# State-space products in 64-token pieces, and one softmax tail moved behind its gate

## The chip, the cores and the metric

One core of a Trainium2 chip runs the kernel. The metric is device time in microseconds (us) of one launch; lower is better. Engines are named as in the profile: PE multiplies matrices (PEld loads its weights), DVE and ACT do most element-wise work, POOL a little of it, SP issues most DMAs. L12 is line 12 of the kernel.

## What is computed

Two decoder layers on 256 tokens of width 2048, float32. The first is a Mamba-2 mixer, the second sliding-window attention with 32 heads in 4 key groups. Cut to what the change touches, the first layer is:

```python
zxbcdt = x @ w_in                                  # z, xs, B, C, dt
xbc = silu(causal_conv(xbc) + conv_b)              # 64 heads of 64; 8 groups, state 128
da = dt * a                                        # chunks of 128 tokens
decay_in = exp(segsum(da))                         # lower triangle of tokens x tokens
cb = einsum("bcqgn,bcsgn->bgcqs", C, B)
y = einsum("bgcqs,bgrcqs,bcsgrp->bcqgrp", cb, decay_in, xs * dt)  # + the carried state
y = (y + xs * d_skip) * silu(z)
y = y * rsqrt(mean over the group's 512 columns of y*y + eps) * norm_w
x = layernorm(ALPHA * x + y @ w_out)
```

and the second, with q, k, v, gate from projections of x:

```python
p = exp(s - m); p = p / (sum(p) + exp(sink - m))   # window of 128 keys
x = layernorm(ALPHA * x + ((p @ v) * silu(gate)) @ w_out)
```

## The kernel before

Products of activations with weights are done on float32 numbers split into two parts: ACT makes the high part of a weight slice (`wh`, L178), DVE the low part (`wl`, L181), and PE adds three products (L265 for projections, 256 token columns each; L339 for the output products, 512 columns each). These run through nearly the whole kernel, 16 steps to a block of 128 projection columns, with four PSUM buffers in turn (the products with v in layer two take from the same four).

The first layer goes through 8 groups. A group g has ten blocks: B, C, four of xs, four of z. Tables by block number (`plan`, `between`, `beside`) say after which block the small steps of a group are written into the program. A scheduler keeps the relative order where the code pins an instruction, and otherwise sets it. The 256 tokens are treated as one triangle of two 128-token pieces. The steps of a group are:

- `load_decay`: DMAs broadcast the running sums of four heads (a half group) over 128 partitions into `rb`; POOL issues five of them (groups 0 to 2), SP the other eleven.
- `sum_decay`, `exp_decay`: ACT makes the decay `e`, 1536 columns for each half group: eight Relu instructions (L566), one exponential (L573).
- `cb`: PE multiplies B with C (L607, L608); DVE masks it (L609). `by_cb`: DVE multiplies it into `e` (L614).
- `turn_first` (group 0; DVE L629) or `turn_xs`, `carry_xs`, `scale_xs`: xs with tokens on partitions, times dt, in `xd`.
- `ymm`: PE multiplies `xd` with `e` (L670). For each pair of column blocks one PSUM tile is filled and DVE evacuates it into `yz` (L675), then adds the skip term (L681).
- `gate`: POOL multiplies by z, squares, and sums the squares (L686, L688, L692); ACT and DVE split the result (L700, L701). The four blocks go in the order 0, 1, 2, 3. `norm` begins with a sum over partitions on PE (L724).

Layer two goes through `B_ORDER`: q(j), g(j) and o(j) are the query, gate and output products of key group j. Each attends in two halves h. After scores and exponentials (L1248) comes the softmax tail, `rest`: DVE's `weigh` (L1252 to L1255) and the transpose in `turn_far` (L1262), whose result ACT moves for the product with v (L1281). `gate_block` makes four blocks p of a gate: PE, ACT's tanh (L1185), then DVE's product (L1186), which also sets the PSUM buffer free. The tail is written at once, except where the table `BEHIND_HALF` delays it: (3, 0) goes behind the first gate product of its key group.

## Time and profile before

| what | value |
|---|---|
| median of 3 runs (lowest to highest) | 975.44 us (975.06 to 976.07) |
| profiled execution: its own time, its span | 975.83 us, 973.8 us |
| granted clock of PE | 1.00 |
| busy: PE, DVE, ACT, POOL | 99%, 81%, 69%, 12% |
| moved by DMA | 197.90 MB, 203 GB/s |

The profile shows one execution. The 2.0 us between its time and its span lie around the program. PE's matmuls are pipelined: the duration of one is longer than the distance from its start to the next start, so costs on PE are read from starts.

### The profile page before, as it was taken

The page shows a single profiled execution, that of the slowest core. Times are in us where ns is not written, and L with a number is a line of the kernel's source. Part 1 is how long each engine was busy: PE and PEld are TensorE (multiplying, and loading weights), DVE is VectorE, ACT ScalarE, POOL GpSimd, SP SyncE. Part 2 cuts the span into 40 slices and gives each one's busy share as a digit, 9 for nine tenths or more (in the row PEclk, how much of TensorE's full clock was granted, in tenths as well). Part 3 has the DMA queues.
Part 4 walks back from the last instruction along what each step waited for, and adds up shares of the span by engine and source line. Part 5 has one row for each costly group of instructions (what it writes and reads, how often), then busy time and mean ns, then how long its engine had stood idle before and what let it go on. Part 6 is the DMA issues. An engine that isn't in the chain of part 4 may idle for free.

```text
span 973.8 us, 18857 instructions
## 1 busy us (share of the span) xinstructions
PE 965.5 (99%) x7332; PEld 892.0 (92%) x7332; DVE 786.6 (81%) x1217; ACT 671.4 (69%) x1282; POOL 119.1 (12%) x202
## 2 busy tenths in 40 slices
PE   9999999999999999999999999999999999999998
PEld 8999989998999999999899899888999988898976
DVE  7978898896977877787797687889977769778778
ACT  7675884884785686487477579467777776884772
POOL 0000403102110310310300121411000000000002
PEclk9999999999999999999999999999999999999999
DMA  9689467676656666576476654568654545456542
GB/s 359 237 290 337 147 216 228 212 230 203 218 192 220 205 205 206 167 237 213 152 250 203 216 178 155 187 190 265 193 174 158 185 138 186 153 177 213 205 143 86
DMA packets 61273, 197.90 MB, mean 203 GB/s; under 512 B 6800, under 2 KB 11328, under 8 KB 60928
## 3 DMA queue, kind: packets, MB, share of 16 engines
q1 hardware_dynamic: 58528, 188.53, 59.1%
q0 software_dynamic: 2048, 7.65, 2.4%
q8 instruction: 57, 0.93, 0.4%
q10 hardware_dynamic: 608, 0.52, 0.2%
q14 instruction: 32, 0.26, 0.1%
HBM read 194.45 MB, written 2.23 MB: 202 GB/s over the span
## 4 chain that ended last, share of the span: by engine, by line
PE 75%; DVE 10%; ACT 6%; DMA 5%; issue 3%; SPq 1%; DVEq 0%; ACTq 0%
PE mm L265 48%; PE mm L339 20%; DVE wl L181 4%; DMA wr<-in_wa 2%; PE mm L1052 2%; PE ax L670 2%; ACT wh L178 2%; DMA wr<-in_wb 1%; ACT p L1248 1%; DMA xr<-in_first 1%; DVE cv L510 1%; ACT e L566 1%; ACT ptw L1281 1%; ACT pt L1281 0%; DMA rscr<-f 0%
## 5 line engine op out<-in xcount | busy, mean ns | idle before, releaser
L181 DVE TENSOR_TENSOR wl<-wr,wh 128x1024 fp32r<-128x1024 f32 (+2 forms) x354 | 391.5, 1126 | 87.8 <-ACT wh L178 86.0
L178 ACT ACTIVATE wh<-wr 128x1024 fp32r<-128x1024 f32 (+2 forms) x354 | 332.9, 974 | 95.9 <-PE mm L265 50.9
L265 PE MATMUL mm<-xH,wh 128*128 128x256 f32 x1280 | 354.6, 277 | 0.1
L265 PE MATMUL mm<-xH,wl 128*128 128x256 f32 x1280 | 353.8, 276 | 0.0
L265 PE MATMUL mm<-xL,wh 128*128 128x256 f32 x1280 | 353.7, 276 | 0.0
L265 PEld LDWEIGHTS mm<-xH,wh 128*128 128x128 f32 x1280 | 240.3, 188 | 2.3 <-issue 1.0
L265 PEld LDWEIGHTS mm<-xL,wh 128*128 128x128 f32 x1280 | 240.4, 188 | 1.0
L265 PEld LDWEIGHTS mm<-xH,wl 128*128 128x128 f32 x1280 | 240.3, 188 | 0.1
L265 PE MATMUL mm<-x1H,wh 128*128 128x256 f32 x512 | 142.2, 278 | 2.1 <-DVE sg L1186 2.1
L265 PE MATMUL mm<-x1L,wh 128*128 128x256 f32 x512 | 141.6, 277 | 0.0
L265 PE MATMUL mm<-x1H,wl 128*128 128x256 f32 x512 | 141.5, 276 | 0.0
L339 PE MATMUL mm<-wh,yH 128*128 128x512 f32 x256 | 100.8, 394 | 0.1
L339 PE MATMUL mm<-wh,yL 128*128 128x512 f32 x256 | 99.8, 390 | 0.0
L339 PE MATMUL mm<-wl,yH 128*128 128x512 f32 x256 | 99.7, 390 | 0.0
L265 PEld LDWEIGHTS mm<-x1H,wh 128*128 128x128 f32 x512 | 96.1, 188 | 3.6 <-DVE sg L1186 2.4
L265 PEld LDWEIGHTS mm<-x1L,wh 128*128 128x128 f32 x512 | 96.2, 188 | 0.1
L265 PEld LDWEIGHTS mm<-x1H,wl 128*128 128x128 f32 x512 | 96.2, 188 | 0.0
L510 DVE SCALAR_TENSOR_TENSOR cv<-mm,pc,cv 128x255 f32<-128x255 f32 x144 | 68.4, 476 | 4.6 <-ACT cv L508 2.5
L686 POOL TENSOR_TENSOR yz<-yz,z 128x256 f32<-128x256 f32 x32 | 26.7, 843 | 259.2 <-DVE yz L681 259.2
L339 PEld LDWEIGHTS mm<-wl,yH 128*128 128x128 f32 x256 | 48.1, 188 | 10.3
L339 PEld LDWEIGHTS mm<-wh,yH 128*128 128x128 f32 x256 | 48.1, 188 | 9.7 <-issue 0.3
L339 PEld LDWEIGHTS mm<-wh,yL 128*128 128x128 f32 x256 | 48.1, 188 | 9.0
(247 smaller groups left out, 1262.8 us busy)
## 6 DMA issues: line engine op xcount, KB each, us to landing
wr<-in_wa SPq DMA_DIRECT2D x154, 512.0 KB, 5.2
wr<-in_wo SPq DMA_DIRECT2D x64, 512.0 KB, 4.4
wr<-in_wq SPq DMA_DIRECT2D x32, 512.0 KB, 4.4
wr<-in_wg SPq DMA_DIRECT2D x31, 512.0 KB, 4.8
wr<-in_wb SPq DMA_DIRECT2D x16, 512.0 KB, 4.0
wr<-in_wb SPq DMA_DIRECT2D x32, 256.0 KB, 4.3
rb<-rscr SPq DMA_DIRECT2D x11, 512.0 KB, 5.4
wr<-in_wkv SPq DMA_DIRECT2D x8, 512.0 KB, 5.7
```

The costliest lines, as they stand in the source:

```text
L178: m = nc.scalar.activation(h[:, sl], v, AF.Copy)
L181: m = nc.vector.tensor_tensor(l[:, sl], v, h[:, sl].bitcast(F32), ALU.subtract)
L265: m = nc.tensor.matmul(ps, a, b, start=first and i == 0, stop=last and i == 2)
L339: pinned(nc.tensor.matmul(ps, a[:, k, hs], (u.h, u.l)[l][:, ks], start=n == 0 and add is None, stop=n == 11), pin)
L510: nc.vector.scalar_tensor_tensor(a[:, sft:], ps[:, : S - sft], w(3 - sft), a[:, sft:], ALU.mult, ALU.add)
L566: m = nc.scalar.activation(e[:, h, cols], rb[:, h, c * P :], AF.Relu, scale=-1.0, bias=rtk[:, c, h0 + h : h0 + h + 1])
L670: nc.tensor.matmul(ps[64 * r : 64 * r + 64, cols], st.xd[:, c, i, 64 * r : 64 * r + 64], e[:, 256:] if c else e[:, :256], start=c == 0, st ...
L686: nc.gpsimd.tensor_tensor(v, v, st.z[i][:], ALU.mult)
L1052: m = nc.tensor.matmul(ps[:], (x1H, x1L, x1H)[i][:, kk, hs], (u.h, u.h, u.l)[i][:, ks], start=(kk, i) == (0, 0), stop=ui == 3 and (k, i) = ...
L1248: nc.scalar.activation(byhead[:, r], byhead[:, r], AF.Exp, bias=ng[:, r : r + 1], accum_out=rs[:, r : r + 1])
L1281: nc.scalar.copy(to[32 * c : 32 * c + 32].rearrange("p r a -> p (r a)"), src[32 * i : 32 * i + 32, cc_].rearrange("p r b -> p (r b)"),)
```

## The change

The tokens of a group are cut into 64-token pieces c = 0 to 3 for the products with the decay. Piece c meets only the tokens from 64c on, so it has 256, 192, 128 or 64 columns (`PART`).

- `ymm`: 32 matmuls of 64 rows by 64 columns of the PE array instead of 16 of 128 rows by 64. The row half is r (the head pair's upper or lower part of the array), the column half b. Both PSUM tiles, one for each r, are complete only after the last product; DVE evacuates blocks 0 and 2, then 1 and 3. The gates follow in the order 0, 2, 1, 3.
- `cb`: four matmuls instead of two, two masks on 64 partitions by 320 columns instead of one on 128 by 384, and two new POOL copies of 64 by 320 to the other half of the partitions. `by_cb` waits for these.
- `sum_decay`: still eight Relu instructions for a half group, now of 256, 192, 128 and 64 columns. `exp_decay` and `by_cb` go over 1280 columns instead of 1536.
- `load_decay`: two DMAs of 64 partitions instead of one of 128, with half the bytes in all, into own halves of `rb`.
- `turn_dt` (once): four ACT copies instead of one, one small exponential and one small product more. `turn_first`: eight products on 64 partitions instead of four on 128. `carry_xs`: as many copies as before to other places.
- `BEHIND_HALF` holds (2, 0) instead of (3, 0): the tail of the third key group's first half stands behind the first gate product of its key group; that of the fourth is written at once.

The core of the diff:

```diff
+PART = [slice(a, a + 256 - 64 * c) for c, a in enumerate((0, 320, 512, 256))]
-BEHIND_HALF = [(1, 1), (3, 0)]
+BEHIND_HALF = [(1, 1), (2, 0)]
...
     def load_decay(g, hf):
-        rb = ap.tile([P, 4, S], F32, tag="rb", name=nm("rb"), bufs=2)
+        rb = ap.tile([P, 2, 2, S], F32, tag="rb", name=nm("rb"), bufs=2)
...
+        for r in range(2):
+            m = (nc.sync if sp else nc.gpsimd).dma_start(
+                rb[64 * r : 64 * r + 64, 0],
+                rscr[h0 + 2 * r : h0 + 2 * r + 2, :]
...
     def cb(g):
...
-        nc.tensor.matmul(ps[:, :256], st.bt[:, :128], st.ct[:], start=True, stop=True)
-        nc.tensor.matmul(ps[:, 256:384], st.bt[:, 128:], st.ct[:, 128:], start=True, stop=True)
-        nc.vector.tensor_tensor(cbm[:], ps[:, :384], mask_ssd, ALU.mult)
+        for c, half, to in ((0, 0, 0), (1, 64, 0), (2, 64, 192), (3, 0, 256)):
+            nc.tensor.matmul(
+                ps[half : half + 64, to : to + 256 - 64 * c], st.bt[:, 64 * c : 64 * c + 64], st.ct[:, 64 * c :],
+                start=True, stop=True,
+            )
+        for r in range(2):
+            rows, at = slice(64 * r, 64 * r + 64), slice(320 * r, 320 * r + 320)
+            nc.vector.tensor_tensor(cbm[rows, at], ps[rows, :320], mask_ssd[rows], ALU.mult)
+        for r in range(2):
+            rows, at = slice(64 * r, 64 * r + 64), slice(320 * r, 320 * r + 320)
+            nc.gpsimd.tensor_copy(cbm[64 - 64 * r : 128 - 64 * r, at], cbm[rows, at])
...
     def ymm(g):
...
+        pss = [ax_tile(), ax_tile()]
         for k in range(2):
-            ps = ax_tile()
-            for i in (2 * k, 2 * k + 1):
-                o = (i % 2) * S
-                for c in range(2):
-                    cols = slice(o + c * P, o + S)
-                    for r in range(2):
-                        e = es[g, i // 2][:, 2 * (i % 2) + r, :]
+            for c in range(4):
+                for r in range(2):
+                    rows = slice(64 * r, 64 * r + 64)
+                    for b in range(2):
                         nc.tensor.matmul(
-                            ps[64 * r : 64 * r + 64, cols], st.xd[:, c, i, 64 * r : 64 * r + 64], e[:, 256:] if c else e[:, :256],
-                            start=c == 0, stop=c == 1,
+                            pss[r][64 * b : 64 * b + 64, k * S + 64 * c : k * S + S], st.xd[rows, k, b, c],
+                            es[g, k][rows, b, PART[c]], start=c == 0, stop=c == 3,
                         )
...
-        for i in range(4):
+        for i in (0, 2, 1, 3):
             at(y, gate, g, i)
...
-            (behind_gate if j == 3 else halves).append(rest)
+            (behind_gate if j == 2 else halves).append(rest)
```

What this makes of the order is shown at three places. The first is PE at the products of group 0; `ax` are the PSUM tiles, `e` the decay of a half group, `mm` the projection blocks. Before:

```order
L265 MATMUL mm_1251<-xH,wl_1092 128x256
L670 MATMUL ax_1310<-e_792,xd_1150 64x256 x2
L670 MATMUL ax_1310<-e_792,xd_1150 64x128 x2
L670 MATMUL ax_1310<-e_792,xd_1150 64x256 x2
L670 MATMUL ax_1310<-e_792,xd_1150 64x128 x2
L670 MATMUL ax_1322<-e_871,xd_1150 64x256 x2
```

And with the change, on PE at the same place:

```order
L265 MATMUL mm_1270<-xH,wl_1107 128x256
L683 MATMUL ax_1329<-e_800,xd_1165 64x256 x2
L683 MATMUL ax_1330<-e_800,xd_1165 64x256 x2
L683 MATMUL ax_1329<-e_800,xd_1165 64x192 x2
L683 MATMUL ax_1330<-e_800,xd_1165 64x192 x2
L683 MATMUL ax_1329<-e_800,xd_1165 64x128 x2
L683 MATMUL ax_1330<-e_800,xd_1165 64x128 x2
L683 MATMUL ax_1329<-e_800,xd_1165 64x64 x2
L683 MATMUL ax_1330<-e_800,xd_1165 64x64 x2
L683 MATMUL ax_1329<-e_879,xd_1165 64x256 x2
```

The first tile was written by the first half group alone; now both tiles are written by each half group, in four products (two rows) for every piece.

The second place is DVE behind these products, where `cv` is the convolution of the next xs block, `el` the carried-in decay, and `yz` the group's y. Before:

```order
L510 SCALAR_TENSOR_TENSOR cv_1301<-mm_1251,pc,cv_1301 128x255
L675 TENSOR_TENSOR yz_1309<-ax_1310,el_943 128x512
L510 SCALAR_TENSOR_TENSOR cv_1301<-mm_1251,pc,cv_1301 128x254
L681 SCALAR_TENSOR_TENSOR yz_1309<-xs_712,pc,yz_1309 128x256
L510 SCALAR_TENSOR_TENSOR cv_1301<-mm_1251,pc,cv_1301 128x253
L681 SCALAR_TENSOR_TENSOR yz_1309<-xs_786,pc,yz_1309 128x256
L675 TENSOR_TENSOR yz_1309<-ax_1322,el_943 128x512
```

And with the change, on DVE behind the products of group 0:

```order
L511 SCALAR_TENSOR_TENSOR cv_1320<-mm_1270,pc,cv_1320 128x255
L181 TENSOR_TENSOR wl_1474<-wr_1477,wh_1473 128x1024
L511 SCALAR_TENSOR_TENSOR cv_1320<-mm_1270,pc,cv_1320 128x254
L511 SCALAR_TENSOR_TENSOR cv_1320<-mm_1270,pc,cv_1320 128x253
L689 TENSOR_TENSOR yz_1328<-ax_1329,el_951 128x2x256
L517 SCALAR_TENSOR_TENSOR xs_1319<-xs_1319,cv_1320 128x256
L695 SCALAR_TENSOR_TENSOR yz_1328<-xs_715,pc,yz_1328 128x256
L695 SCALAR_TENSOR_TENSOR yz_1328<-xs_870,pc,yz_1328 128x256
L689 TENSOR_TENSOR yz_1328<-ax_1330,el_951 128x2x256
```

The first evacuation stands behind a whole `wl` and all of the convolution.

The third place is DVE at the first gate block of key group 2; `sg` is the gate, `sm` and `p` belong to the softmax. Before:

```order
L181 TENSOR_TENSOR wl_9960<-wr_9961,wh_9959 128x896
L1252 TENSOR_TENSOR sm_9821<-sm_9821 128x8
L1253 RECIPROCAL sm_9821<-sm_9821 128x8
L1254 TENSOR_SCALAR sm_9821<-sm_9821 128x8
L1255 TENSOR_TENSOR p_9808<-p_9808,sm_9821 128x8x4x32
L181 TENSOR_TENSOR wl_9960<-wr_9963,wh_9959 128x1024
L1262 STREAM_TRANSPOSE z_9839<-p_9808 128x1024
L1186 SCALAR_TENSOR_TENSOR sg_9891<-sg_9891,mm_9904 128x256
```

And with the change, on DVE at that gate block:

```order
L181 TENSOR_TENSOR wl_10150<-wr_10151,wh_10149 128x896
L181 TENSOR_TENSOR wl_10150<-wr_10153,wh_10149 128x1024
L1200 SCALAR_TENSOR_TENSOR sg_10079<-sg_10079,mm_10092 128x256
L1266 TENSOR_TENSOR sm_10015<-sm_10015 128x8
L181 TENSOR_TENSOR wl_10289<-wr_10290,wh_10288 128x128
L1267 RECIPROCAL sm_10015<-sm_10015 128x8
L181 TENSOR_TENSOR wl_10289<-wr_10290,wh_10288 128x896
L1268 TENSOR_SCALAR sm_10015<-sm_10015 128x8
L181 TENSOR_TENSOR wl_10289<-wr_10292,wh_10288 128x1024
L1269 TENSOR_TENSOR p_10002<-p_10002,sm_10015 128x8x4x32
L1276 STREAM_TRANSPOSE z_10147<-p_10002 128x1024
```

The gate product now stands ahead of the five instructions of the tail, and the next unit's three `wl` are spread among them.

More of the change, by code (lines that the diff above doesn't have):

```diff
@@ L411, in first_products @@
         return pss
[L414 to L415 removed]
+    dtx = ap.tile([P, NHD // 2, 4], F32, tag="dtx", name="dtx")
+    dtq = ap.tile([P, 2, 2, 8], F32, tag="dtq", name="dtq")
+    rtk = ap.tile([P, 2, 3, 2, NHD // 2], F32, tag="rtk", name="rtk")
     rscr = dram.tile([P, S], F32, tag="rscr", name="rscr")
```

105 lines of the change are left out of this document (53 added, 52 removed).

## The prediction

> **What bounds the kernel now.** I read the page first, then the chain, PE's waits, and the timeline at the places that the change touches.
>
> ```profile
> PE 965.5 (99%) x7332; PEld 892.0 (92%) x7332; DVE 786.6 (81%) x1217; ACT 671.4 (69%) x1282; POOL 119.1 (12%) x202
> PE 75%; DVE 10%; ACT 6%; DMA 5%; issue 3%; SPq 1%; DVEq 0%; ACTq 0%
> L670 PE MATMUL ax<-e,xd 128*64 128x256 f32 x128 | 19.6, 385 | 0.0
> L670 PE MATMUL ax<-e,xd 128*64 128x128 f32 x128 | 12.4, 273 | 0.0
> ```
>
> PE is busy 99% of the span and carries 75% of the chain. DVE (81%) and ACT (69%) have room on the whole, so what they save counts only where PE waits for them. These are PE's waits over the span, by line, releaser, total, times and longest:
>
> ```profile
> PE mm L265 <- DVE sg L1186: 2.1, 1, 2.1
> PE ax L388 <- DVE zero L376: 1.0, 1, 1.0
> PE ax L724 <- POOL sq L692: 0.3, 1, 0.3
> ```
>
> Two of the three lie where the change works: the gate product and the sum of squares. So there are two ways to gain: fewer PE cycles in eight visits to the products, and the 2.1 us wait. There is one evident way to lose, at L724.
>
> **The products on PE.** The timeline of PE at group 1's products and at the attention scores (columns: start, time, operation), the second being the nearest operation with four 64 by 64 tiles:
>
> ```profile
> 141.95 2.82 PE L670 MATMUL ax<-e,xd 128*64 128x256 f32 x32
> 144.70 0.50 PE L339 MATMUL mm<-wh,yH 128*128 128x512 f32 x1
> ...
> 733.35 1.53 PE L1220 MATMUL ax<-kT,qT 64*64 64x192 f32 x32
> 734.81 0.39 PE L265 MATMUL mm<-x1H,wh 128*128 128x256 f32 x1
> ```
>
> Each float32 matmul is two records. A visit to L670 is 32 records; with two column tiles working side by side that makes 16 pairs, eight of 256 and eight of 128 columns, 3072 columns in a row, and lasts 144.70 - 141.95 = 2.75 us. L1220 has 32 records; if four tiles work side by side that is eight quartets of 192, 1536 columns in a row, in 734.81 - 733.35 = 1.46 us. The difference, 1.29 us for 1536 columns, is 0.84 ns a column, and 0.17 us is left for entering and leaving in both. If only pairs overlapped in L1220, its 3072 columns would need 2.75 us as L670 does; so there they do overlap in fours.
>
> The new visit has 64 records, 16 quartets: for each of two k and two passes 256 + 192 + 128 + 64 = 640 columns, 2560 in all. At 0.84 ns that is 2.15 + 0.17 = 2.32 us, 0.43 us less than now. No row has a quartet of 64 columns. The nearest that tells what a short matmul costs is the four one-column matmuls of L724:
>
> ```profile
> 106.45 0.28 PE L265 MATMUL mm<-xH,wl 128*128 128x256 f32 x1
> 106.99 0.61 PE L724 MATMUL ax<-cc,sq 128*128 128x1 f32 x4 [0.26 <-POOL sq L692]
> 107.46 0.68 PE L607 MATMUL ax<-ct,bt 128*128 128x256 f32 x2
> ```
>
> They take 107.46 - 106.99 = 0.47 us, 0.118 each, however few the columns. Were that a floor for a quartet, the four of 64 columns would cost 0.064 more than their 0.054 and the four of 128 columns 0.010 more than their 0.108: 0.30 us a visit, which leaves a gain of 0.13. L724 loads 128 by 128 weights, twice the columns of these tiles, so I take the middle: -0.3 us a visit, between -0.43 and -0.13. In group 0 it is swallowed by the wait below, so seven visits count: -2.1 us (-3.0 to -0.9).
>
> On that floor the Trainium skill, TensorEngine Tiling (Array Packing), Instruction Overhead, speaks against this change: a matmul carries about 60 cycles of overhead on TRN2, one with a free dimension of 1 lasts as long as one with 60, and a tiling factor should not be taken from a dimension that is already small. Pieces of 64 columns are at that limit. The 0.118 us of L724 agrees that short matmuls have a floor; no run here shows it for four tiles.
>
> `cb` streams 256 + 128 columns through the whole array before; after, each column half takes 320 (256 + 64 and 192 + 128), side by side as the pairs of L670. At 0.84 ns that is 0.05 us less, against entering another tile shape (part of the 0.17 above): I take zero.
>
> **The wait at L724.** DVE and POOL behind group 0's products:
>
> ```profile
> 94.14 0.48 DVE L510 SCALAR_TENSOR_TENSOR cv<-mm,pc,cv 128x255 f32<-128x255 f32 x1
> 94.53 0.68 DVE L675 TENSOR_TENSOR yz<-ax,el 128x512 f32<-128x512 f32 x1
> 95.13 0.47 DVE L510 SCALAR_TENSOR_TENSOR cv<-mm,pc,cv 128x254 f32<-128x254 f32 x1
> 95.52 0.47 DVE L681 SCALAR_TENSOR_TENSOR yz<-xs,pc,yz 128x256 f32<-128x256 f32 x1
> ...
> 96.08 0.73 POOL L686 TENSOR_TENSOR yz<-yz,z 128x256 f32<-128x256 f32 x1 [23.47 <-DVE yz L681]
> ...
> 101.48 0.91 POOL L686 TENSOR_TENSOR yz<-yz,z 128x256 f32<-128x256 f32 x1 [0.37 <-DVE yz L681]
> ...
> 106.19 0.74 POOL L692 TENSOR_TENSOR sq<-sq,sq 128x256 f32<-128x256 f32 x1
> ```
>
> POOL's gates begin when the first skip term ends (95.99) and end at 106.93, and PE waits for that: without it L724 would start about 0.11 after 106.45, so 0.42 us are lost now. With the change the first evacuation follows 255 columns of convolution (to 94.53), one `wl` (1.14 from start to start), the 254 and 253 columns (0.39 each), its own 0.60, an xs product (0.35) and the skip term (0.47): 97.9 us, 1.9 later. POOL has 0.37 us of waiting for DVE inside the chain, and DVE's remaining steps come closer together, since both evacuations are ready at once. So I take 0.7 off and 1.2 us for POOL's end and for PE behind it. The bounds are 0, if DVE is through its queue early enough to keep the old start, and 2.2, if nothing is caught up and the extra instructions of `turn_first`, next, still push DVE by 0.3.
>
> `turn_first` issues eight products on half the partitions instead of four:
>
> ```profile
> 81.50 1.41 DVE L629 TENSOR_TENSOR xd<-ax,dtx 128x256 f32<-128x256 f32 x4
> ...
> L609 DVE TENSOR_TENSOR cbm<-ax,cc 128x384 f32<-128x384 f32 x8 | 4.4, 545 | 0.0
> L614 DVE TENSOR_TENSOR e<-e,cbm 128x1536 f32<-128x1536 f32 x16 | 27.9, 1746 | 3.4 <-ACT e L573 3.3
> L573 ACT ACTIVATE e<-e 128x1536 f32<-128x1536 f32 x16 | 23.6, 1478 | 0.0
> L534 POOL DMA_DIRECT2D rb<-rscr x5: 528/545/719, 43.1 to 118.6; - x5
> ```
>
> As each goes over as many columns as before, that adds 1.3 to 1.4 us to DVE once, ahead of the products of group 0. It is the reason for the upper bound above.
>
> **The steps off PE.** By columns, L614 goes from 1746 to 1455 ns, sixteen times, and L573 from 1478 to 1232; the mask of 545 ns becomes two of 320 columns, about 0.47 each, +0.4 us eight times. In groups 2 to 7 none of this counts: PE waits for none of it now, as the list above shows, and the products come several blocks after `e` is ready. The new POOL copies cost 0.5 to 1.0 us each by POOL's nearest rows (the 0.73 and 0.91 of L686 with 128x256), and POOL is busy 12%. The halved `rb` costs one more issue for each load: five more on POOL at 0.55 us, ahead of POOL's gates, and eleven on SP ahead of the weights' loads; both run blocks ahead of the use. `turn_dt`'s extra copies (about 1.4 us of ACT) lie in the DMA-bound start. All zero; if the cover were gone, the largest single step is the two copies, about 1.5 us, in group 1.
>
> Group 1 is where DVE's columns do count:
>
> ```profile
> 130.11 0.28 PE L265 MATMUL mm<-xH,wl 128*128 128x256 f32 x1
> 130.46 0.50 PE L339 MATMUL mm<-wh,yH 128*128 128x512 f32 x1
> ...
> 135.85 0.39 PE L339 MATMUL mm<-wl,yH 128*128 128x512 f32 x1
> 136.31 0.36 PE L265 MATMUL mm<-xH,wh 128*128 128x256 f32 x1
> ```
>
> L265 starts normally follow after 0.11 us and L339 after 0.23; here 0.35 and 0.46, so 0.47 us are lost while DVE is late with z and the layer's sums. DVE saves 0.6 there and adds 0.4, and PE comes later by the wait at L724: -0.4 us (-0.5 to 0).
>
> **The softmax tail.** PE, DVE and ACT at the gate of key group 2:
>
> ```profile
> 832.09 1.48 PE L1220 MATMUL ax<-kT,qT 64*64 64x192 f32 x32
> 831.12 0.17 DVE L1252 TENSOR_TENSOR sm<-sm 128x8 f32<-128x8 f32 x1 [1.49 <-ACT p L1248]
> 832.90 1.22 DVE L181 TENSOR_TENSOR wl<-wr,wh 128x1024 fp32r<-128x1024 f32 x1
> 834.04 1.24 DVE L1262 STREAM_TRANSPOSE z<-p 128x1024 f32<-128x1024 f32 x1
> 835.20 0.38 DVE L1186 SCALAR_TENSOR_TENSOR sg<-sg,mm 128x256 f32<-128x256 f32 x1
> 832.14 0.36 ACT L1185 ACTIVATE sg<-mm 128x256 f32<-128x256 f32 x1
> 859.43 1.23 DVE L181 TENSOR_TENSOR wl<-wr,wh 128x1024 fp32r<-128x1024 f32 x1 [0.71 <-ACT wh L178]
> ```
>
> ACT's tanh is done at 832.50, but the product that frees the first block's PSUM buffer stands behind the tail until 835.20. Two gate blocks and two products with v have taken the four buffers by then, so PE's third block waits for it: the 2.1 us of the list. With the change it follows the `wl` (1.14 from start to start), which can run once ACT's part of it is made, from about 832.0 to 833.2, and ends near 833.6. PE's scores end near 833.5 (832.09 + 1.46). So about 2.0 us of wait go. Late next: behind the product, the tail and the next unit's `wl` share DVE, some 3 us (1.14 + 1.16 + three small ones) later than now. DVE's wait in the last row shows 0.71 us free there; a `wl` standing behind a transpose (1.16), a gate product (0.34) and a mask could keep PE waiting up to 0.7. I take -1.4 us (-2.1 to -0.3).
>
> The tail of (3, 0) is now immediate, in front of a gate product on DVE. That product ended at 904.83; three more us there are covered, since the buffer that it frees is needed only when PE is through the second block, whose tanh follows at 913.91:
>
> ```profile
> 904.42 0.41 DVE L1186 SCALAR_TENSOR_TENSOR sg<-sg,mm 128x256 f32<-128x256 f32 x1
> 913.91 0.38 ACT L1185 ACTIVATE sg<-mm 128x256 f32<-128x256 f32 x1
> ```
>
> **Sum.** -2.1 + 1.2 - 0.4 - 1.4 = -2.7 us on the profiled 975.83, so 973.1. That run was 0.4 above the median of 975.44; from the median it is 972.7. All favourable ends give -3.0 + 0 - 0.5 - 2.1 = -5.6 (969.8), all unfavourable -0.9 + 2.2 + 0 - 0.3 = +1.0 (976.4).
>
> **Rivals.**
> *Only pairs overlap (slower).* L1220's order alternates between row halves, while the new loop goes through the column halves of one row half first. If the four did not overlap, a visit would take 5120 columns at 0.84 ns and 0.17, 4.47 us, 1.72 more than now. Eight visits make +13.8; with the other terms (+1.2 - 0.4 - 1.4) the time is 988.6. It decides from a visit above 2.75 us. For it: no row shows this order. Against: L1220's fours.
> *Short pieces have a floor.* At 0.118 us for a quartet the products gain only 0.9: -0.9 + 1.2 - 0.4 - 1.4 = -1.5, 973.9, within what can be told. The page named above gives this mechanism its reason.
> *Waits take the place of waits.* The sum of squares is late by the full 2.2 and the attention pays back all but 0.3: -2.1 + 2.2 - 0.4 - 0.3 = -0.6, 974.8. For it: both stand in queues without slack. Against: PE's list has just one such wait in the attention.
> That the change does not do what it says I give nothing: the order shows the gate product ahead of the tail.
>
> **Chances.** The forecast has 0.60, the pairs 0.18, the floor 0.11, the swapped waits 0.11. A measurement of this kernel tells about 0.2%, 1.95 us, from no change. So faster 0.60, same 0.22, slower 0.18. The range from 969.8 to 976.4 takes in all the bounds and the two middle rivals, and leaves out the pairs.
>
> **What would show it.** Right: L683 to the next line's start about 2.45 us in each group, L724 starting near 108.2, no wait of PE for sg at 833, and PE's next waits under 1 us. Wrong: visits of 4.5 us (pairs), visits of 2.6 (floor), L724 past 109 or a new PE wait for `wl` near 858 (swapped waits).

## The result: slower by 0.3%

| kernel | median of 7 runs | lowest to highest |
|---|---|---|
| before | 975.23 us | 974.91 to 976.13 |
| changed | 978.05 us | 976.95 to 980.47 |

The ratio is 1.0031 (95% interval 1.0019 to 1.0043). The prediction of 972.7 us, with a range up to 976.4, was wrong, and its sign too. The runs of the changed kernel also spread over 3.5 us, those of before over 1.2. The profiled execution is the slowest of the seven: 980.47 us with a span of 978.7, so it shows more loss than the median.

The page of the changed kernel, busy time first, then the shares of the chain:

```profile
PE 967.8 (99%) x7620; PEld 897.1 (92%) x7620; DVE 786.1 (80%) x1230; ACT 664.9 (68%) x1286; POOL 125.4 (13%) x223
PE 80%; ACT 6%; DVE 5%; issue 4%; DMA 3%; POOL 1%; ACTq 0%; SPq 0%; DVEq 0%; POOLq 0%
```

PE is busy 2.3 us longer although it multiplies fewer columns. PE's waits of the changed kernel (line, releaser, total, times, longest):

```profile
PE ax L738 <- POOL sq L706: 2.7, 1, 2.7
PE mm L339 <- DVE xr L350: 1.9, 1, 1.9
...
PE mm L265 <- DVE wl L181: 0.2, 1, 0.2
```

The wait for `sg` is gone as forecast. The wait for the sum of squares (L724 before, L738 now) has grown from 0.3 to 2.7 us, and a wait of 1.9 us is new: an output product of o(1) (L339) waits for DVE to free a PSUM buffer (L350). PE's timeline in the changed kernel at the places that matter:

```profile
108.11 0.28 PE L265 MATMUL mm<-xH,wl 128*128 128x256 f32 x1
111.08 0.61 PE L738 MATMUL ax<-cc,sq 128*128 128x1 f32 x4 [2.69 <-POOL sq L706]
...
146.85 2.41 PE L683 MATMUL ax<-e,xd 64*64 64x256 f32 x64
149.19 0.51 PE L339 MATMUL mm<-wh,yH 128*128 128x512 f32 x1
...
835.04 1.48 PE L1234 MATMUL ax<-kT,qT 64*64 64x192 f32 x32
836.61 0.39 PE L265 MATMUL mm<-x1H,wh 128*128 128x256 f32 x1
...
880.88 0.39 PE L339 MATMUL mm<-wl,oH 128*128 128x512 f32 x1
883.17 0.57 PE L339 MATMUL mm<-wh,oH 128*128 128x512 f32 x1 [1.90 <-DVE xr L350]
883.54 0.63 PE L339 MATMUL mm<-wh,oL 128*128 128x512 f32 x1
883.97 0.63 PE L339 MATMUL mm<-wl,oH 128*128 128x512 f32 x1
```

A visit to the products lasts 149.19 - 146.85 = 2.34 us. In the last two rows the step from one start to the next is 0.43 us, where the same instruction normally follows after 0.23: behind the wait PE runs at half its clock. The windows of the changed kernel show it behind both waits (window, length, PE busy, granted clock, DMA share, GB/s):

```profile
112.00:118.00 6.00, 6.00 (x26) 0.72 0.57 198
884.00:888.00 4.00, 4.00 (x13) 0.64 0.72 261
```

Time in which PE is busy at 0.72 or 0.64 of its clock is part of why the busy time rose. Set side by side, PE's starts in the two profiled executions give the whole balance; the last column is how far the changed kernel is behind by then:

| PE reaches | before | changed | behind |
|---|---|---|---|
| group 0's products, start | 87.37 | 89.43 | +2.06 |
| group 0's products, end | 90.12 | 91.77 | +1.65 |
| the norm's sum (L724, L738) | 106.99 | 111.08 | +4.09 |
| the first L265 behind it | 113.67 | 119.45 | +5.78 |
| group 1's products, start | 141.95 | 146.85 | +4.90 |
| group 2's products, start | 232.79 | 237.94 | +5.15 |
| group 7's products, end | 613.37 | 616.28 | +2.91 |
| scores at key group 2's gate | 832.09 | 835.04 | +2.95 |
| next L265 | 835.64 | 836.61 | +0.97 |
| last L339 ahead of the new wait | 879.15 | 880.88 | +1.73 |
| end of o(1) | 884.91 | 890.44 | +5.53 |
| last matmul (L1453, L1467) | 967.39 | 971.88 | +4.49 |
| span | 973.8 | 978.7 | +4.9 |

So the two waits with the half clock behind them cost 2.44 + 1.7 and 2.06 + 1.7 us, the way to group 0's products 2.06, and against that stand eight visits at -0.41, -1.98 at the old wait and -0.9 in group 1. That makes +3.8 of the +4.9; the rest is spread (+0.66 between groups 1 and 2, +0.76 between the gate and o(1), +0.7 in small steps, -1.04 near the end).

### The profile page after: what moved, and what is told of

Its sections match the earlier page's. It is cut to its first block, busy times and chain, and to the rows that moved or that the text cites. A ratio compares the mean times of both kernels' runs of the same rounds, so it can differ in the third digit from the quotient of the medians.

```text
span 978.7 us, 19519 instructions
## 1 busy us (share of the span) xinstructions
PE 967.8 (99%) x7620; PEld 897.1 (92%) x7620; DVE 786.1 (80%) x1230; ACT 664.9 (68%) x1286; POOL 125.4 (13%) x223
## 4 chain that ended last, share of the span: by engine, by line
PE 80%; ACT 6%; DVE 5%; issue 4%; DMA 3%; POOL 1%; ACTq 0%; SPq 0%; DVEq 0%; POOLq 0%
PE mm L265 49%; PE mm L339 25%; PE mm L1066 2%; DVE wl L181 2%; ACT wh L178 2%; DMA wr<-in_wa 2%; PE ax L683 2%; DMA xr<-in_first 1%; ACT p L1262 1%; PE ax L610 1%; ACT ptw L1295 1%; ACT pt L1295 0%; DMA first<-in_first 0%; PE ax L1227 0%; PE ax L1234 0%
## 5 line engine op out<-in xcount | busy, mean ns | idle before, releaser
L265 PE MATMUL mm<-xH,wh 128*128 128x256 f32 x1280 | 356.2, 278 | 0.0
L265 PE MATMUL mm<-xL,wh 128*128 128x256 f32 x1280 | 355.1, 277 | 0.0
L265 PE MATMUL mm<-xH,wl 128*128 128x256 f32 x1280 | 355.1, 277 | 0.0
L265 PEld LDWEIGHTS mm<-xH,wh 128*128 128x128 f32 x1280 | 240.9, 188 | 1.9 <-issue 0.3
L265 PEld LDWEIGHTS mm<-xL,wh 128*128 128x128 f32 x1280 | 241.0, 188 | 1.0
L265 PEld LDWEIGHTS mm<-xH,wl 128*128 128x128 f32 x1280 | 241.2, 188 | 0.0
L265 PE MATMUL mm<-x1H,wh 128*128 128x256 f32 x512 | 142.4, 278 | 0.1
L265 PE MATMUL mm<-x1H,wl 128*128 128x256 f32 x512 | 141.8, 277 | 0.2 <-DVE wl L181 0.2
L265 PE MATMUL mm<-x1L,wh 128*128 128x256 f32 x512 | 141.8, 277 | 0.0
L339 PE MATMUL mm<-wh,yH 128*128 128x512 f32 x256 | 101.5, 397 | 0.0
L339 PE MATMUL mm<-wh,yL 128*128 128x512 f32 x256 | 100.4, 392 | 0.0
L339 PE MATMUL mm<-wl,yH 128*128 128x512 f32 x256 | 100.4, 392 | 0.0
L265 PEld LDWEIGHTS mm<-x1H,wh 128*128 128x128 f32 x512 | 96.2, 188 | 1.6 <-issue 0.6
L265 PEld LDWEIGHTS mm<-x1H,wl 128*128 128x128 f32 x512 | 96.3, 188 | 0.4 <-DVE wl L181 0.4
L265 PEld LDWEIGHTS mm<-x1L,wh 128*128 128x128 f32 x512 | 96.2, 188 | 0.1
L714 ACT ACTIVATE yH<-yz,pc 128x256 fp32r<-128x256 f32 x32 | 16.3, 510 | 70.3 <-POOL yz L700 70.3
L339 PEld LDWEIGHTS mm<-wl,yH 128*128 128x128 f32 x256 | 48.4, 189 | 10.2
L339 PEld LDWEIGHTS mm<-wh,yH 128*128 128x128 f32 x256 | 48.5, 189 | 9.8
```

The source lines that it names most:

```text
L265: m = nc.tensor.matmul(ps, a, b, start=first and i == 0, stop=last and i == 2)
L339: pinned(nc.tensor.matmul(ps, a[:, k, hs], (u.h, u.l)[l][:, ks], start=n == 0 and add is None, stop=n == 11), pin)
L714: nc.scalar.activation(yH[:, i, :], v, AF.Copy, scale=pc[:, c : c + 1])
```

## The experiments

Each kernel was timed in 7 to 12 executions beside the kernel before on the same chip, except two that were executed once. There were four such sets, each on another chip; the median of before was 975.33 to 975.46 in all four.

**The two parts alone.** First, before with the softmax tail moved and nothing else:

```diff
-BEHIND_HALF = [(1, 1), (3, 0)]
+BEHIND_HALF = [(1, 1), (2, 0)]
...
-            (behind_gate if j == 3 else halves).append(rest)
+            (behind_gate if j == 2 else halves).append(rest)
```

> The kernel before with the softmax-tail edit alone. If the moved tail is what costs in the output products of key group 1 (waits theory), the wait of 2.4 us on PE before the third gate block of key group 2 goes (-2.0), and a wait of about 2 us on PE for L350 near 879 appears, with PE at part of its clock behind it (another 0 to 1.9): 975.0 to 977.0 in all. If the tail edit does what was forecast and the loss comes from the products (products theory), 973.3 to 974.2, and no such wait.

Measured: 976.63 us (975.48 to 981.57), ratio 1.0022 (1.0011 to 1.0032). The tail's move makes the kernel slower by itself. PE's waits of this kernel:

```profile
PE mm L339 <- DVE xr L350: 1.9, 1, 1.9
...
PE mm L265 <- ACT wh L212: 0.2, 1, 0.2
PE mm L339 <- DVE wl L181: 0.2, 1, 0.2
```

The 2.1 us at the gate became 1.9 us in o(1), some 45 us later, and two small ones. Here the clock stayed full behind the wait:

```profile
879.00:883.00 4.00, 3.77 (x16) 1.00 0.93 298
```

Second, the changed kernel with the old `BEHIND_HALF`, so the pieces alone (the reverse of the diff above):

> The changed kernel with the softmax tails as before, so the 64-token products alone. Waits theory: products -3.3, cb +1.6, the wait at the sum of squares +2.4 and 0 to 1.6 of part clock behind it, group 1 -0.8: 975.1 to 977.0. Rival (four tiles at once draw the clock down everywhere): starts of L265 3% apart from normal in many stretches, 977 or more. If the tail were the only loss: 973 or less.

Measured: 977.51 us (974.13 to 979.57), ratio 1.0030 (1.0019 to 1.0041). So the pieces lose too, and spread over 5.4 us. (The tail alone stays within 2.6 us but for one execution of 981.57.) By the medians the parts cost 1.3 and 2.2 us beside before, and the whole change 2.8. The profiled execution is the fastest of this kernel, 974.13, and its waits have no L738:

```profile
PE mm L265 <- DVE sg L1200: 2.1, 1, 2.1
...
```

**Each once more**, one execution with no edit, to see whether a longer execution differs by that wait. The pieces alone:

> The second run once more, for another profile, since its first profile was its fastest execution. Waits theory: an execution near the median shows the wait at the sum of squares (1.5 to 3 us) and weights landing later near 50 to 60 us than in the first profile.

Measured: 978.54 us, with the wait:

```profile
PE mm L265 <- DVE sg L1200: 2.1, 1, 2.1
PE ax L738 <- POOL sq L706: 1.8, 1, 1.8
...
```

And the changed kernel:

> The changed kernel once more, for another profile. Waits theory: the wait for L350 at the output products of key group 1 is there again, about 2 us; the wait at the sum of squares is 0 to 3 us and goes with the time.

Measured: 976.18 us, without it:

```profile
PE mm L339 <- DVE xr L350: 1.9, 1, 1.9
...
```

Of the four profiled executions of these two kernels, the two with the wait at L738 took 978.54 and 980.47, the two without it 974.13 and 976.18. It comes and goes from run to run in the same program. What varies ahead of it is when DVE comes to group 0's `xd`: 82.98 and 82.59 us in the two profiles with the wait, 79.15 and 78.25 in the two without. Weights that arrive at another time go with that. The last ACT step that waits for a DMA ahead of it started at 60.09 us in the changed kernel (first row) and at 55.38 in the first profile of the pieces alone (second row); in the other two profiles it is 59.71 with the wait and 56.28 without. From 62 to 100 us DVE idles only 2.5 us, so little of such a delay is made up. That the weights are the cause is not shown: in the kernel with the shortened sum, below, DVE came to `xd` late, at 81.97, and ACT's last such wait had ended at 50.88.

```profile
60.09 1.06 ACT L178 ACTIVATE wh<-wr 128x1024 fp32r<-128x1024 f32 x1 [2.26 <-DMA wr<-in_wa]
```

```profile
55.38 1.06 ACT L178 ACTIVATE wh<-wr 128x1024 fp32r<-128x1024 f32 x1 [2.25 <-DMA wr<-in_wa]
```

**Is it DVE's extra work in group 0?** In the pieces alone, PE turns group 0's xs with 16 matmuls against the identity, straight onto the right partitions, so that DVE has two products of 128 by 512 instead of eight on 64 partitions:

```diff
+            for q in range(4):
+                for r in range(2):
+                    nc.tensor.matmul(
+                        ps[64 * r : 64 * r + 64, q * P : (q + 1) * P], st.xs[2 * k + r][:, 64 * q : 64 * q + 64], ident,
+                        start=True, stop=True,
+                    )
+            m = nc.vector.tensor_tensor(st.xd[:, k], ..., ALU.mult)
```

> As the second run, but group 0's xs is turned by PE straight into the new places (sixteen products with the identity, 64 rows each, instead of eight transposes), so DVE needs two products of 128 by 512 instead of eight of 64 by 256, and the small product and exponential for them go. PE pays about 0.9 us for it, DVE saves about 2.1 ahead of group 0's products. Waits theory: the wait at the sum of squares shrinks by about 2 to 0.5-1.0 us and no part clock follows: 1 to 2.5 us below the second run. If DVE's lateness there has another cause, the wait stays above 2 us and the time is 0 to 1 above the second run.

Measured: 975.89 us (975.08 to 976.33), ratio 1.0008 (0.9999 to 1.0017): 1.6 us less than the pieces alone, and the spread is gone. The two sides of the trade, DVE's products in this kernel and in the changed kernel:

```profile
80.83 1.28 DVE L635 TENSOR_TENSOR xd<-ax,dtx 128x512 f32<-128x512 f32 x2
```

```profile
82.98 3.55 DVE L641 TENSOR_TENSOR xd<-ax,dtq 64x256 f32<-64x256 f32 x8
```

The eight products took 3.55 us, where I had put twice the 1.41 of before. One of them lasts as long as one of before (421 and 416 ns on average), but they follow each other at 0.45 us instead of 0.33.

**The lateness without the pieces.** Before, with its four products cut into eight on 64 partitions:

```diff
+                for q in range(2):
+                    rows = slice(64 * q, 64 * q + 64)
-                    st.xd[:, :, i, :]..., ps[:, o : o + S]..., dtx[:, ...]
+                    st.xd[rows, :, i, :]..., ps[rows, o : o + S]..., dtx[rows, ...]
```

> The kernel before with group 0's four products of 128 by 256 on DVE (L629) made as eight of 64 by 256, and nothing else. Waits theory: DVE is 2.1 us later from 83 us on and has no idle time to catch up, so the wait at the sum of squares (L724) grows from 0.4 to about 2 us: 976.5 to 978.5. If the late evacuation order alone made that wait in the changed kernel: 975.2 to 975.8.

Measured: 975.65 us (974.39 to 978.88), ratio 1.0006 (0.9998 to 1.0015). This expectation failed. The eight products lasted 3.52 us here too, but PE's wait stayed as it was:

```profile
PE ax L726 <- POOL sq L694: 0.3, 1, 0.3
```

But POOL's sum did end 0.64 us later than in before (107.57 against 106.93). PE was late by the same 0.64 in this execution, from 20 us on, so the wait did not grow. DVE's 2.1 us reach POOL in part, and alone they made no long wait here. The other half is PSUM tiles that are complete only after the last product, so that the first evacuation comes behind the convolution. In the profiled execution of the changed kernel that is the DVE and then the POOL timeline:

```profile
96.81 0.48 DVE L511 SCALAR_TENSOR_TENSOR cv<-mm,pc,cv 128x255 f32<-128x255 f32 x1
97.20 1.21 DVE L181 TENSOR_TENSOR wl<-wr,wh 128x1024 fp32r<-128x1024 f32 x1
98.34 0.99 DVE L511 SCALAR_TENSOR_TENSOR cv<-mm,pc,cv 128x254 f32<-128x254 f32 x2
99.25 0.68 DVE L689 TENSOR_TENSOR yz<-ax,el 128x512 f32<-128x512 f32 x1
100.22 0.88 DVE L695 SCALAR_TENSOR_TENSOR yz<-xs,pc,yz 128x256 f32<-128x256 f32 x2
```

```profile
100.84 0.86 POOL L700 TENSOR_TENSOR yz<-yz,z 128x256 f32<-128x256 f32 x1 [25.77 <-issue]
109.97 1.06 POOL L706 TENSOR_TENSOR sq<-sq,sq 128x256 f32<-128x256 f32 x1
```

The first evacuation starts at 99.25 instead of 94.53, and POOL's chain at 100.84 instead of 96.08. From there POOL needs 10.19 us to 111.03 where before took 10.85 (96.08 to 106.93), so it makes up 0.66 of 4.76 us; the rest, 4.10, is what the norm's sum starts later on PE.

**Is it that wait?** In the pieces alone, the sum that PE waits for in group 0 holds the first block only, so the sums of the other three squares are missing from the group's normalisation:

```diff
+        elif g == 0 and i == 2:
+            st.rest = q
         else:
-            nc.gpsimd.tensor_tensor(st.ss[:], st.ss[:], q[:], ALU.add)
+            to = st.rest if g == 0 else st.ss
+            nc.gpsimd.tensor_tensor(to[:], to[:], q[:], ALU.add)
```

> The second run, but the sum of squares of group 0 that PE waits for holds the first block alone; the other three are added into a tile that nobody reads (this part of the computation is left out). All of POOL's and DVE's work stays. Waits theory: PE no longer waits there, and the median falls from 977.5 to 974.0-975.5, with a spread as narrow as in the third run. If the wait is not what makes the second run's median and spread: 976.5 to 978.

Measured: 975.79 us (974.65 to 979.12), ratio 1.0007 (0.9998 to 1.0016), 1.7 us below the pieces alone, but with a spread that stayed wide, which the expectation had not. So the wait at the norm, with what follows it, is worth 1.7 us in the median, and does not make the whole spread. In its profiled execution (977.38) DVE's lateness came out elsewhere, at `cv` (the row for `sg` is the old wait at the gate):

```profile
PE mm L265 <- DVE sg L1203: 2.0, 1, 2.0
PE mm L265 <- DVE cv L511: 1.7, 1, 1.7
...
PE mm L339 <- DVE cv L511: 0.6, 1, 0.6
```

**The slow stretches.** Behind `cb` of group 0, PE's L265 follow each other at 117.8 ns instead of 113.4 for some 14 us, at a granted clock of 1.00. The first row is before, the second the changed kernel:

```profile
61.00:76.00 15.00, 15.00 (x135) 1.00 0.73 241
```

```profile
61.00:76.00 15.00, 15.00 (x130) 1.00 0.77 251
```

Fewer matmuls fit into the same full window. The first suspect is `cb` in column halves, so one kernel lets `cb` go over the whole array in two matmuls again, with masks and POOL copies to suit:

```diff
+        nc.tensor.matmul(ps[:, :256], st.bt[:, :128], st.ct[:], start=True, stop=True)
+        nc.tensor.matmul(ps[:, 256:384], st.bt[:, 128:], st.ct[:, 128:], start=True, stop=True)
+        for r, at, of, w in ((0, 0, 0, 384), (1, 384, 64, 192), (1, 576, 320, 64)):
+            ...
+            nc.vector.tensor_tensor(cbm[rows, at : at + w], ps[rows, of : of + w], cc[rows, m : m + w], ALU.mult)
```

> As the second run, but B times C in two products over the whole array as before (256 and 128 columns), masked in three pieces of 384, 192 and 64 columns, with the columns of the decay in another order. If the four small products cost 0.2 us in each of eight groups, 1.6 us below the second run; if not, within 0.3 of it.

Measured: 977.32 us (976.47 to 978.2), ratio 1.0023 (1.0013 to 1.0034), within 0.2 us of the pieces alone; the 1.6 us did not come. The window behind `cb` did become fast, but another one became slow, and DVE's later `cv` cost PE 1.5 us:

```profile
61.00:76.00 15.00, 15.00 (x135) 1.00 0.81 250
44.00:59.00 15.00, 15.00 (x130) 1.00 1.02 327
```

```profile
PE mm L264 <- DVE sg L1195: 2.1, 1, 2.1
PE mm L264 <- DVE cv L510: 1.5, 1, 1.5
...
```

The second suspect is the address from which the next projection step reads its tokens. The program keeps a second copy of the first token tile and reads it between plain blocks, but not behind the places on a list (`visits`). With PE turning xs, this kernel takes `cb` and `turn_first` off that list, so that the step behind them reads the second copy:

```diff
-    visits = (turn_dt, cb, turn_first, ymm, norm)
+    visits = (turn_dt, ymm, norm)
```

> The third run with one more edit: after B times C and after the turning of group 0, the first projection step reads the second copy of the first token tile (at another address), as the kernel does between plain blocks. In the profiles with 64-token pieces whole stretches of L265 (60 to 77, 77 to 90, 178 to 190 us) start 117.8 ns apart instead of 113.4. If which of the two rates a stretch takes is set where it is entered, by the first address, these stretches come back to 113.4 or others turn slow: a change of 0.5 to 1.5 us from the third run. If the four-tile products set it, the stretches stay at 117.8 and the time within 0.3 us.

Measured: 975.93 us (975.09 to 977.32), ratio 1.0007 (0.9999 to 1.0016), the same as with the list. The stretch behind the turning became fast, the one behind `cb` stayed slow. Over all 16 profiles, PE loses 0.83 us against before from 58 to 75 us in each of the eight with `cb` in column halves, 0.25 of it at `cb`, and at most 0.04 in the seven others with `cb` over the whole array. So in group 0 the slow rate comes with the column halves. But it also comes at places without them: between 9 and 19 us it is there in the profile of the next kernel, whose first layer is that of before, and not in before's own. What sets it there stays open.

**Can the tail be moved for less?** Before, with DVE's `weigh` at once and only the transpose behind the gate product:

```diff
+        def part():
+            weigh()
+            behind_gate.append(turn_far)
...
+        elif (j, h) == (2, 0):
+            part()
```

> The kernel before with only the transposes of the tail of (2, 0) behind the gate product; the scaling of p stays ahead of it. Waits theory (the tail's scaling and transposes and the next weights crowd DVE until the output products of key group 1): the wait at the third gate block shrinks by one transpose, 1.2 us, and the transposes come only 0.3 later, so that L350 keeps its place: 974.0 to 974.8. If any delay of the transposes is paid back in full in the output products: 975.0 to 975.6.

Measured: 975.39 us (974.68 to 975.98), ratio 1.0001 (0.9992 to 1.0009):

```profile
PE mm L265 <- DVE sg L1186: 1.4, 2, 0.9
...
PE mm L339 <- DVE xr L350: 0.6, 1, 0.6
```

Half of the move takes 0.7 off the waits for `sg` (2.1 before, now 1.4 in two) and puts 0.6 on L350. The same with the pieces and PE turning xs:

> The third run and the tail split of the sixth together. If the two places are independent the gain of the sixth adds to the third: 974.6 to 975.2; if the tail's gain is paid back: 975.8 to 976.2.

Measured: 976.28 us (975.5 to 977.36), ratio 1.0013 (1.0004 to 1.0021), no better than without it (975.89).

Then POOL instead of DVE scales p of that half, with the transposes behind the gate product; first on before, then on the version below:

```diff
-            nc.vector.tensor_tensor(
+            (nc.gpsimd if (j, h) == (2, 0) else nc.vector).tensor_tensor(
                 byhead, byhead, ri.unsqueeze(2).unsqueeze(3).to_broadcast([P, 8, 4, 32]), ALU.mult
...
+            behind_gate.append(lambda: later(1, turn_far, 0))
```

> The same edit on the kernel before. If the wait is worth its 2.1 us: 973.0 to 974.0; with part clock behind it in some executions of before, more. If it is paid back later: 975.0 to 976.0.

Measured: 976.04 us (975.53 to 978.76), ratio 1.0011 (1.0002 to 1.0020), slower by 0.1%, just clear of its interval. The waits for `sg` did not go; they grew from 2.1 to 2.4 us:

```profile
PE mm L265 <- DVE sg L1186: 2.4, 2, 1.7
```

DVE and POOL side by side in it show why:

```profile
831.25 2.87 DVE L181 TENSOR_TENSOR wl<-wr,wh 128x1024 fp32r<-128x1024 f32 x1 [0.34 <-ACT wh L178]
...
831.14 1.90 POOL L1255 TENSOR_TENSOR p<-p,sm 128x1024 f32<-128x1024 f32 x1 [140.20 <-ACT p L1248]
```

A `wl` that takes 1.22 us alone took 2.87 beside POOL's product: about POOL's time and then its own. The Trainium skill, SBUF — State Buffer, Who interferes with whom, says that a DVE instruction with two SBUF inputs contends with a GpSimd one that reads SBUF, that the shared ports are an exclusive lock, and that the order of issue decides who blocks; these rows agree (POOL began 0.11 us ahead).

> The ninth run with the tail's scaling of (2, 0) on POOL and its transposes behind the first gate product, so that DVE neither holds that product back nor gets the work later. If the wait there (2.1) and the part clock behind it (1.6 in three profiles) hold back the gain: 971.5 to 973.5. If the freed wait is paid back at the output products of key group 1 as with the moved tail: 974.5 to 976.

Measured: 976.67 us (974.98 to 978.5), ratio 1.0013 (1.0005 to 1.0022), slower as well and above both expected ranges. It has the same waits for `sg` (2.4 us in two).

**The best that the runs pointed to**: the pieces, PE turning xs, `cb` over the whole array, and the tail where it was.

> The third and the fourth run together (group 0 turned by PE, B times C over the whole array), and the second copy of the first token tile only behind the turning. If the losses are where the profiles put them (B times C with its slow stretches about 1.5, the slow stretch behind the turning 0.4, no wait at the sum of squares): 973.3 to 974.5, below both kernels. If the four-tile products' gain of 3.3 is lost elsewhere: 975 or more.

Measured: 975.06 us (974.1 to 978.4), ratio 1.0002 (0.9993 to 1.0012). It is about 3 us below the changed kernel and level with before; the expected 973.3 to 974.5 was not reached. Its profiled execution (974.66) has no wait at the norm, but the old wait at the gate is followed by a slow clock, which it was not in the profile of before (first row this version, second before):

```profile
833.00:837.00 4.00, 3.41 (x20) 0.72 0.72 231
```

```profile
835.00:839.00 4.00, 3.36 (x29) 1.00 0.70 209
```

## Why the prediction was wrong, step by step

**The products: right, and better than taken.** The visit fell from 2.75 to 2.34 us, the favourable end (2.32). 2560 columns at 0.84 ns and 0.17 us explain it, short pieces included. So the pairs (a visit of 4.5) and the floor (2.6) fall. The overhead that the prediction cites from the Trainium skill (TensorEngine Tiling (Array Packing), Instruction Overhead) does not show for 64-column pieces on four tiles; these lie just above the page's 60, and no run here has shorter ones. The sum's -2.1 was -3.3 in the profile: the swallowed visit of group 0 counts as well, since PE's earlier arrival is part of how its wait is measured.

**The norm's wait: the mechanism was right, its size was not, and its consequence was missing.** The sum had +1.2, at most 2.2; the profiled execution lost 2.44 against before, and L738 started at 111.08, not near 108.2. The way on DVE, from the start of group 0's `xd` to POOL's first gate, shows which steps failed:

| profile | `xd` starts | to POOL's first gate | POOL's sum ends | PE's wait |
|---|---|---|---|---|
| before | 81.50 | 14.58 | 106.93 | 0.26 |
| before with eight products | 80.96 | 15.74 | 107.57 | 0.26 |
| pieces, PE turning xs | 80.83 | 15.99 | 106.40 | none |
| pieces alone | 78.25 | 17.84 | 105.68 | none |
| pieces alone, again | 82.59 | 17.86 | 110.00 | 1.78 |
| changed, again | 79.15 | 17.85 | 106.58 | none |
| changed | 82.98 | 17.86 | 111.03 | 2.69 |

The change makes this way 3.26 to 3.28 us longer in each of its four profiles. For it I had 1.9 for the order of the evacuations and at most 0.3 for `turn_first`. The eight products alone add 1.16, and the order with PE turning xs 0.95 to 1.41 in four profiles, so together they cost more than each by itself. The larger error is in the first: `turn_first` was costed by columns, +1.3 to 1.4, and cost +2.1 (3.55 against 1.41), of which I let 0.3 reach POOL. The other step that failed is that I took DVE's time of arrival at `xd` from one profile as fixed. In these four profiles it varies over 4.7 us, and with it the wait. The 0.7 that I let POOL make up came out (0.66). In the changed kernel's profile 3.28 longer, 1.48 later at `xd` and 0.66 made up by POOL give the 4.10 at the norm's sum; 1.65 of it is PE's own lateness by then. Then PE lost 1.7 more behind the wait, most of it at half clock, a term that no step had. Turning by PE (-1.6, although PE pays 1.1 for it) and the shortened sum (-1.7, although `cv` then makes PE wait) show that this place is worth at least some 1.7 us in the median, in a kernel that sometimes meets the wait and sometimes not.

**The start and `cb`: "all zero" was wrong.** PE came to group 0's products 2.06 us late. Of that, 0.8 arose in the first 20 us, half of it where L265 start 0.21 us apart up to 6.2 us, which in before ends at 5.3. This part is not shown to be the change's: the four profiles of kernels with the first layer of before, or nearly, are 0.3 to 0.64 late there too. But 0.25 arose at `cb`, which takes 0.70 us from start to the next line instead of 0.57 and is entered later, and 1.0 in two stretches at 117.8 ns. Between the products of groups 1 and 2 another `cb` and another such stretch made +0.66 (from +4.90 - 0.41 to +5.15 in the table). I had looked for cover of DVE, POOL and ACT, and for PE's own steps had counted columns only.

**Group 1: -0.9 instead of -0.4, but by luck.** All of before's small waits from 124 to 137 us vanished in the changed kernel. They vanished as well, for the same 0.9 us, in the profiles of the tail alone, of the split tail on before and of POOL's product on before, where group 1 is as in before. So the forecast's cause (DVE's savings, a later PE) is not shown; before's profile had waits that the same code does not always have.

**The softmax tail: here the step that failed is "Late next".** The wait at 833 went, for -1.98. But I put what comes next at up to 0.7 us, from one `wl` with 0.71 of room at 859. What PE needs next is not only a `wl` but L350, the evacuation that frees a PSUM buffer for the fifth block of o(1). DVE in before, then in the changed kernel:

```profile
878.45 0.67 DVE L350 TENSOR_TENSOR xr<-xr,mm 128x512 f32<-128x512 f32 x1
```

```profile
881.32 1.20 DVE L181 TENSOR_TENSOR wl<-wr,wh 128x1024 fp32r<-128x1024 f32 x1
882.44 0.68 DVE L350 TENSOR_TENSOR xr<-xr,mm 128x512 f32<-128x512 f32 x1
```

In before L350 ended at 879.12 and PE needed the buffer at 879.37: 0.25 us of room, and no wait on the list that would have pointed there. With the change it ended 4.0 us later while PE was only 1.7 later, so PE waited 2.06; a smaller `wl` wait at 861 (0.41 by PE's starts) came on top.

What sets L350 is a chain of ACT and DVE, not a lack of gaps on DVE, which idles 12.6 us from 836 to 882 in the changed kernel and 11.9 in before, waiting for ACT. ACT in turn waits for the transposed p and makes its copies ahead of the next `wh`; the transpose now comes later (before, then the changed kernel):

```profile
835.31 4.14 ACT L1281 COPY pt<-z 32x256 f32<-32x256 f32 x10 [1.03 <-DVE z L1262]
```

```profile
841.56 3.32 ACT L1295 COPY pt<-z 32x256 f32<-32x256 f32 x8 [3.88 <-DVE z L1276]
```

Counted from the start of the scores at the gate, this chain takes the same time in every profile with the same tail, whether PE runs at full or at half clock behind the gate (us):

| tail of (2, 0) | profiles | to the transpose | to L350 |
|---|---|---|---|
| at once | 9 | 1.90 to 1.95 | 46.26 to 46.36 |
| transposes behind the gate product | 2 | 2.27 | 46.94 to 46.95 |
| the same, p scaled by POOL | 2 | 3.06 to 3.08 | 47.45 to 47.47 |
| all behind the gate product | 3 | 5.23 to 5.24 | 47.40 |

So the 2.1 us at the gate were largely slack: PE needed them back at L350. With the chain of before unchanged, an estimate from these rows is that losing the whole wait would have brought PE the 0.25 us of room, and the move made the chain 1.04 us longer. That fits the wait: 1.98 + 1.04, less 0.25 of room and 0.76 that PE lost ahead of it, is 2.0. The tail alone shows it without any half clock: in its profile PE gained 1.98 at the gate and had lost 3.5 again by the last matmul (976.63 in the median, slower). The half move paid back 0.6 for 0.7. That is the rival "waits take the place of waits", to which I gave 0.11; even it was too mild, since I let the attention pay back all but 0.3 and it paid back more than it had gained, with 1.7 us of half clock in the profiled execution. About 1.0 came back at the end, where before's small gaps in PE between 947 and 953 us were no longer there. This goes with the pieces and not with the tail: the pieces alone have it (-1.25), the tail alone does not (+0.1); how the one brings the other is not shown.

**The half clock.** Ten of the 18 waits between 1.5 and 2.7 us in all these profiles, the two in the changed kernel among them, were followed by it: windows of 4 us from the wait's end show a clock of 0.57 to 0.72. It followed none of the four up to 1.74 us and ten of the fourteen from 1.78 us up; the wait for `sg` of 2.0 to 2.1 us was followed by it in six of the profiles and not in three, before among these. The profile of before is thus not typical: of 101 executions of before timed beside these kernels (one of 2796 us left out), 58 had a mean granted clock of 0.997 or 0.998, with a median of 975.51 us, and 43 one of 0.999 or 1.000, with 974.93. Where no wait is as long (both kernels with the split tail, and POOL's product on before) all 33 had 0.999 or 1.000, and with POOL's product on the best version 10 of 11. So in these kernels, their start aside, the half clock came only behind waits of about 1.8 us and more, and not behind all of them; what decides it is not shown. In the profiles PE lost 1.5 to 1.8 us by it, while before's executions with the lower mean clock are only 0.6 us longer than the others. That late engines catch up meanwhile would explain this and is not shown. The Trainium skill, TensorE: Matmul & The Clock Gate, What's actually happening, states a half and a full clock, switched by a free-running activity window of about 3.4 us, with one idle window as the condition for the half; its next section (Wait — 56ns, not 53.3ns?) gives 426.7 ns for 512 columns at the half. The trace agrees on rate and length: starts 0.43 us apart from 883.54 to 886.92, which is 3.4 us. It differs on the condition: the waits here are shorter than such a window.

**What stays open.** What sets the rate of 117.8 or 113.4 ns of a stretch of L265, other than `cb` in column halves. What moves DVE's arrival at `xd` from run to run. And what before and the best version differ in beyond the profiles: in that version's profile PE gains 0.41 us at each of the eight visits, one after the other, loses 1.1 by turning xs on PE (1.90 us from its start to the next line, against 0.79), 0.4 at the start and 0.4 in a slow stretch, and is 2.05 us ahead of before's profile at the gate, of which the half clock takes 1.63. Over all runs it is level; which of these terms vary from run to run was not taken apart.

## What to carry to other kernels

The wait of 2.1 us that stood on the list was worth, here, no more than the room at the next place where PE met the other engines. So before removing a wait, follow the chain of the other engines from there to every later consumer, also to those that are on no list because they were just in time: the chain of ACT and DVE to L350 took 46.3 us whatever PE did, and PE had 0.25 us of room there. When work is added on an engine with little idle time (here DVE, 3.3 us on the way to POOL's gate), whether it costs anything can depend on when that engine arrives, which varies from run to run, so one profile does not show the room. Gaps in a single profile of before can also be gone in the next one without any change. And here a PE wait of 1.8 us or more could bring some 3.4 us at half clock behind it, which four shorter waits did not.

## What the runs showed of the hardware

- Pieces of 64 columns on four 64 by 64 tiles cost by columns: 2560 columns in 2.34 us.
- A DVE product of 256 columns lasted 421 ns on 64 partitions and 416 ns on 128; eight of the first took 3.55 us and four of the second 1.41. Halving the partitions saved nothing, and here the products also followed each other less closely.
- PE's clock was granted at half for about 3.4 us behind ten of fourteen waits of 1.78 to 2.69 us, and behind none of four from 1.53 to 1.74 us.
- At a full granted clock, one and the same loop of 128x256 matmuls ran at 113.4 or at 117.8 ns each, the slow rate for some 7 to 14 us at a time in the first layer.
- DVE's `wl`, with both inputs in SBUF, took 2.87 instead of 1.22 us beside a POOL product of 1.90 that began 0.11 us ahead.
